# A fifth group of seven products in the second FFN projection, and the PLE product moved ahead of its gate

## Chip, cores and metric

The kernel runs on one core of a Trainium2 chip. The metric is the time of one execution on the device in microseconds (us), lower is better; a kernel's time is the median of several executions.

## What is computed

One layer of an encoder over 1024 tokens of width 1024, all in float32. In short:

```python
hn = rmsnorm(h, norm_mix_g);  z = hn @ w_in            # pooling mixer and chunked attention
h  = h + concat([a, o]) @ w_out
hn = rmsnorm(h, norm_ffn_g);  up = hn @ w_up           # 1024 x 5632
gt, val = up[..., :2816], up[..., 2816:]
gt = causal_dwconv(gt, conv_w, conv_b)                 # width 3
h  = h + (gelu(gt) * val) @ w_down                     # 2816 x 1024, the second projection
hn = rmsnorm(h, norm_ple_g)
gate = sigmoid(hn @ w_ple_gate + b_ple_gate)
h  = h + gate * (p @ w_ple)                            # p is 1024 x 256, the PLE product
out = rmsnorm(h, final_g)
```

The change concerns the second projection and what follows it.

## The kernel before

**Products.** Everything lies transposed: features on the 128 partitions, tokens along the free axis. Each float32 operand is split into a high part (ACT copies it to the type `fp32r`) and a low part (DVE subtracts); `split` (L132 to L134) does both. A product of two operands is three matmuls, high x high, high x low, low x high (`mm3`, L128 to L130). A token half is 512 columns, a PSUM bank; PSUM has eight banks.

**First projection.** The 2816 features are 22 tiles of 128, `fi` = 0 to 21. For each tile gate and value columns are computed together by seven products in the manner of Strassen instead of eight: steps `n` in the order (1, 5, 6, 2, 7, 3, 4), each 4 x 3 = 12 matmuls. `step(fi, n)` issues one, the text counts them as steps 1 to 7 of a tile by position. DVE forms sums of weight quarters (L700) and ACT and DVE split them, three products ahead. PSUM results are handed from product to product: `keep` copies one out (L785), `seed` copies a bank into another (L789), on which the next product accumulates. After step 6 (`n` = 3) the convolution and GELU run (L834 to L837), after step 7 the value factor (L842 to L851), and the tile's result Y lies in `Yb`. `up(fi, ...)` is one tile; its hooks are things to do between steps.

**Second projection.** The output rows are 8 blocks `H[d]` of 128, two token halves each. Two ways are used:

- *Plain*: for two tiles at a time, each block and half gets 2 x 3 matmuls (`down_mm`), and DVE adds the bank to `H` (`down_add`). Y and the weights `w_down` must be split first.
- *Groups of four tiles*: seven products for eight, over halves of the output features, token halves and pairs of tiles. Y goes to DRAM (`Yd`, L908), and sums of Y blocks and of weight blocks are put together by loading one block and adding others on top in DMAs of the POOL queue (L961), into one of two raw buffers for each kind ("one", "grow"; L963 loads from the SP queue). `ask` issues these loads when a buffer is free and the tiles that are read are stored; `split_next` splits the operands of the next product into the buffers `pairs` (tiles BQ and a part of R), of which there is one set; `down_next` issues one product, 4 x 2 x 3 = 24 matmuls into banks 4 to 7, adds them to H by four DVE instructions (L1008), and calls `split_next` for the next product. `H` holds sums of its quarters meanwhile, formed and undone by DVE.

Before, tiles 0 and 1 are plain (during tile 2), tiles 2 to 17 are four groups, tiles 18 and 19 and tiles 20 and 21 are plain, behind the last tile, accumulated together in PSUM. A group's seven products stand between the steps of the four tiles that follow it; those of the last group in tiles 18 and 19 alone:

```python
        for fi in range(3, 6):
            up(fi, negative(fi))
            if fi == 3:
                split_next()
        for g in range(1, 4):
            for z, fi in enumerate(group_of(g)):
                up(fi, negative(fi), {n: down_next for i, n in enumerate(steps[fi]) if (7 * z + i) % 4 == 1})
        last_at = (1, 4, 6, 8, 10, 12, 13)
```

**Gate.** Behind it come the norm of H, the gate product (8 blocks of 8 x 3 matmuls, for tokens 0 to 511, 512 to 767 and 768 to 1023 in turn), and in each of these 24 rounds, behind the gate product, the PLE product of the same block (`ple_mm`, 2 x 3 matmuls). `gate_out` takes the sigmoid (L1157), multiplies it with the PLE product in PSUM (L1158) and adds to H (L1159). The final norm and the output follow.

**Order.** TensorE executes in the order of the program text. The instructions of the other engines, their DMAs among them, are ordered by a planner when the kernel is built, by the order of the text (`tc.high_priority` moves some ahead) and by its own estimates of when their inputs are there. Each engine then executes its list in order.

Of the kernel before, what the change touches and what calls it, by code (L numbers as in the profile page):

```python
# [6 lines left out]
F32 = mybir.dt.float32  # L7
# [86 lines left out]
def trunk(tc, xT, pT, vecs, w_qk0, w_in, w_v, bias, counts, pool_w, w_out, w_up, w_down,  # L94
# [4 lines left out]
    with tc.tile_pool(name="sb", bufs=1) as sb, \  # L99
# [567 lines left out]
        rawu = [f(2 * s, 512) for s in range(4)] + [f(40, 512)]  # L667
        rawd = f(42, 512)
# [33 lines left out]
        def prepare(upto):  # L702
            while prepared[0] < min(upto, len(order)):
# [3 lines left out]
                fetch(prepared[0] + 2)  # L707
# [158 lines left out]
        b_pool = tc.tile_pool(name="b3", bufs=1)  # L866
        B = b_pool.__enter__().tile([P, 7168], F32R, name="B3")
        gv = [B[:, 2048 * s:2048 * (s + 1)] for s in range(2)]
        wd = [(B[:, 4096:5120], B[:, 5120:6144]), (B[:, 6144:7168], r(60, 1024))]

        def down_weights(fi, dst, raws=(rawd,)):
            for z in range(2):
                t = raws[z % len(raws)]
                sp.dma_start(t, w_down[fi, :, z * 512:(z + 1) * 512])
                split(t, dst[0][:, z * 512:(z + 1) * 512], dst[1][:, z * 512:(z + 1) * 512])

        def down_mm(d, h, bank, ws, gs, first=True, last=True):
            for i in range(2):
                w_, a = ws[i], gs[i]
                mm3(PS[:, bank], w_[0][:, d * P:(d + 1) * P], w_[1][:, d * P:(d + 1) * P],  # L880
                    a[:, h * 512:(h + 1) * 512], a[:, 1024 + h * 512:1024 + (h + 1) * 512],
                    first and i == 0, last and i == 1)
# [3 lines left out]

        def down(tiles, ring):
            for n in tiles:
                d, h = n % KT, n // KT
                bank = ring[n % len(ring)]  # L890
                down_mm(d, h, bank, wd, gv)
                down_add(d, h, bank)

        def up(fi, dst, hooks=None):
# [5 lines left out]
            for n in steps[fi]:  # L900
                step(fi, n)
                if hooks and n in hooks:
                    hooks[n]()
            if isinstance(dst, int):

                values_in(slice(0, SEQ), dst)
                for ts in HS:
                    sp.dma_start(Yd[fi][:, ts], Yb[:, ts])  # L908
                stored.add(fi)
                ask()  # L910
                return
# [5 lines left out]
        def downs(ring):  # L917
            def at(a, b):
                return lambda: down(range(a, b), ring)
            return {6: at(0, 4), 3: at(4, 8), 7: at(8, 12), 4: at(12, 16)}  # L920


        Yd, stored = {}, set()
        raws, pairs = {}, {}
        asked, todo = {}, []
        split_done = set()

        def group_of(g):
            return range(4 * g + 2, 4 * g + 6)
# [12 lines left out]
        def ask():  # L942
# [3 lines left out]
            for side in "wa":  # L946
                for kind in ("one", "grow"):
                    queue = todo_of[side, kind]
                    while queue:
# [5 lines left out]
                        queue.pop(0)  # L955
                        grown = n in (GROWING_W if side == "w" else GROWING_A)[1:]
# [18 lines left out]
        sequence = [(g, n) for g in range(4) for n in DOWN_ORDER]  # L975
# [20 lines left out]
        def down_next():  # L996

            g, n = sequence[ndown[0]]
            ndown[0] += 1
            fresh = n in (1, 5, 6, 7)  # L1000
# [9 lines left out]

        down_weights(0, wd[0])
        up(0, gv[0])
        up(1, gv[1], {7: lambda: down_weights(1, wd[1])})
        d_pool = tc.tile_pool(name="yd", bufs=1, space=bass.MemoryType.DRAM)
        dp = d_pool.__enter__()
        for fi in range(2, NF - 3):
            Yd[fi] = dp.tile([P, SEQ], F32, name=f"Yd{fi}")
        up(2, 1, downs((4, 5, 6, 7)))
        b_pool.__exit__(None, None, None)
        b_pool = tc.tile_pool(name="bq", bufs=1)  # L1020
        bp = b_pool.__enter__()
        B = bp.tile([P, 3072], F32R, name="BQ")
        RW = bp.tile([P, 4096], F32, name="RW")
        spots = [B[:, 1024 * z:1024 * (z + 1)] for z in range(3)] + [r(60, 1024)]
        for s, side in enumerate("wa"):
            for j in range(2):
                p_ = spots[2 * s + j]
                pairs[side, j] = p_[:, 0:512], p_[:, 512:1024]
                for q, kind in enumerate(("one", "grow")):
                    z = 4 * s + 2 * q + j  # L1030
                    raws[side, kind, j] = RW[:, 512 * z:512 * (z + 1)]
        for d in range(4):
            for a, b, op in ((H[4 + d][:, HS[0]], H[4 + d][:, HS[1]], ALU.subtract),
                             (H[d][:, HS[1]], H[4 + d][:, HS[1]], ALU.add)):
                dve.tensor_tensor(a, a, b, op)
        ask()

        def negative(fi):

            return 1 if (fi - 2) % 4 < 2 else 0  # L1040
# [11 lines left out]
        b_pool.__exit__(None, None, None)  # L1052
        b_pool = tc.tile_pool(name="b3t", bufs=1)
        B = b_pool.__enter__().tile([P, 7168], F32R, name="B3T")
        gv = [B[:, 2048 * s:2048 * (s + 1)] for s in range(2)]
        wd = [(B[:, 4096:5120], B[:, 5120:6144]), (B[:, 6144:7168], r(60, 1024))]
        for ts in HS:
            store(gv[1], ts)
        for d in range(4):
            for a, b, op in ((H[4 + d][:, HS[0]], H[4 + d][:, HS[1]], ALU.add),  # L1060
                             (H[d][:, HS[1]], H[4 + d][:, HS[1]], ALU.subtract)):
                dve.tensor_tensor(a, a, b, op)
        for ts in HS:
            sp.dma_start(rawd, Yd[18][:, ts])
            split(rawd, gv[0][:, ts], gv[0][:, 1024 + ts.start:1024 + ts.stop])
        for fi in (18, 19):
            down_weights(fi, wd[fi % 2])
# [3 lines left out]
        wd2 = [(r(8 * s, 1024), r(8 * s + 4, 1024)) for s in range(2)]  # L1071
        banks = (4, 5, 6, 7, 0, 2, 1, 3)

        nl = len(loads)
        raw_last = [(rawu[nl % 5], rawd), (rawu[(nl - 4) % 5], rawu[(nl - 1) % 5])]
        up(last_f[0], None)
        up(last_f[1], gv2[1], {1: lambda: store(gv2[0]),
                             3: lambda: down_weights(last_f[0], wd2[0], raw_last[0]),
                             4: lambda: down_weights(last_f[1], wd2[1], raw_last[1])})


        wg = [r(b, 2048) for b in (44, 52, 16, 24, 96, 104, 80, 88)]
        hp = [[(r(b, 512), r(b + 2, 512)) for b in bs]
              for bs in ((112, 116, 120, 124, 32, 36, 40, 60), (0, 4, 8, 12, 64, 68, 72, 76))]
# [3 lines left out]
        def pair(src, hi, lo):  # L1088
            t = rawg[ng[0] % 3]
            ng[0] += 1  # L1090
            sp.dma_start(t, src)
            split(t, hi, lo)
# [17 lines left out]
        for d in range(KT):  # L1110
            down_mm(d, 0, banks[d], wd, gv, True, False)
        for k in range(KT):
            pair(w_gate[k], wg[k][:, 0:1024], wg[k][:, 1024:2048])
        for d in range(KT):
            down_mm(d, 0, banks[d], wd2, gv2, False, True)
            down_add(d, 0, banks[d])
            norm_a.add(d, pool)
        for d in range(KT):
            down_mm(d, 1, banks[d], wd, gv, True, False)
            if d < 7:  # L1120
                weighted2(0, d)
        weighted2(0, 7)
        b_pool.__exit__(None, None, None)
        v_pool.__exit__(None, None, None)
        b_pool = tc.tile_pool(name="b4", bufs=1)
        B = b_pool.__enter__().tile([P, 8192], F32R, name="B4")
        pt = [B[:, 2048 * k:2048 * (k + 1)] for k in range(2)]
        wp = [B[:, 4096 + 2048 * k:4096 + 2048 * (k + 1)] for k in range(2)]
        for k in range(2):
            pair(pT[k], pt[k][:, 0:1024], pt[k][:, 1024:2048])  # L1130
            pair(w_ple[k], wp[k][:, 0:1024], wp[k][:, 1024:2048])
# [161 lines left out]
```

## Time and profile before

| | us |
|---|---|
| three executions | 1148.33, 1150.03, 1153.02 |
| median | 1150.03 |
| the profiled execution | 1150.81 |
| its span, first to last instruction | 1149.0 |

| engine | busy, us | share |
|---|---|---|
| TensorE (PE) | 1133.6 | 99% |
| VectorE (DVE) | 875.9 | 76% |
| ScalarE (ACT) | 589.8 | 51% |
| GpSimd (POOL) | 139.6 | 12% |

In rows of the profile PE is a matmul and PEld a weight load, "SPq" an issue in SyncE's queue. A row of a timeline begins with start and duration in us; an engine's idle time before the instruction, and what ended it, stand in brackets. In rows by stage each engine has its busy time and number of instructions; the granted TensorE clock, the share of the DMA engines and GB/s follow. Durations of matmuls overlap; the time of one is the distance between two starts. The same holds for DVE and ACT instructions in a row.

In the profiled execution the FFN's first group product starts at 522.41 us, the last at 930.41, and the first gate product at 1022.8. The span ends at 1149.0.

### The profile page before, as it was taken

The page shows a single profiled execution, that of the slowest core. Times are in us where ns is not written, and L with a number is a line of the kernel's source. Part 1 is how long each engine was busy: PE and PEld are TensorE (multiplying, and loading weights), DVE is VectorE, ACT ScalarE, POOL GpSimd, SP SyncE. Part 2 cuts the span into 40 slices and gives each one's busy share as a digit, 9 for nine tenths or more (in the row PEclk, how much of TensorE's full clock was granted, in tenths as well). Part 3 has the DMA queues.
Part 4 walks back from the last instruction along what each step waited for, and adds up shares of the span by engine and source line. Part 5 has one row for each costly group of instructions (what it writes and reads, how often), then busy time and mean ns, then how long its engine had stood idle before and what let it go on. Part 6 is the DMA issues. An engine that isn't in the chain of part 4 may idle for free.

```text
span 1149.0 us, 15722 instructions
## 1 busy us (share of the span) xinstructions
PE 1133.6 (99%) x5747; PEld 963.4 (84%) x5747; DVE 875.9 (76%) x1504; ACT 589.8 (51%) x1035; POOL 139.6 (12%) x179
## 2 busy tenths in 40 slices
PE   8999999999999999999999999999999999999997
PEld 7988998888888878878888888888888878888897
DVE  7678878879657887778787887787878799776543
ACT  8568677765555651444343534453444436645433
POOL 0000000083002100001201120112012200220000
PEclk9999999999999999999999999999999999999999
DMA  7110102104500120545755574557455903600012
GB/s 264 37 49 31 49 12 68 40 28 155 166 19 9 56 74 31 151 130 138 173 139 156 147 174 129 156 147 174 129 156 147 219 1 110 195 26 1 10 65 74
DMA packets 58975, 115.93 MB, mean 101 GB/s; under 512 B 6673, under 2 KB 7953, under 8 KB 58897
## 3 DMA queue, kind: packets, MB, share of 16 engines
q1 hardware_dynamic: 47232, 93.88, 24.2%
q0 software_dynamic: 11520, 20.98, 11.4%
q8 instruction: 45, 0.74, 0.3%
q14 instruction: 34, 0.27, 0.1%
q10 hardware_dynamic: 144, 0.07, 0.0%
HBM read 101.79 MB, written 13.11 MB: 100 GB/s over the span
## 4 chain that ended last, share of the span: by engine, by line
PE 92%; issue 3%; DVE 2%; ACT 2%; DMA 0%; SPq 0%; POOL 0%; POOLq 0%; DVEq 0%; ACTq 0%
PE PS L128 28%; PE PS L129 28%; PE PS L130 28%; PE PS L367 2%; PE PS L385 1%; PE PS L384 1%; PE PS L342 1%; PE PS L341 1%; DMA F<-in_w_qk 0%; PE PS L350 0%; PE PS L349 0%; PE PS L617 0%; ACT F L353 0%; DVE B L375 0%; DVE BQ L134 0%
## 5 line engine op out<-in xcount | busy, mean ns | idle before, releaser
L128 PE MATMUL PS<-R 128*128 128x512 f32 (+1 forms) x1144 | 430.1, 376 | 3.3 <-ACT PS L789 1.4
L130 PE MATMUL PS<-R 128*128 128x512 f32 (+1 forms) x1144 | 425.1, 372 | 0.0
L129 PE MATMUL PS<-R 128*128 128x512 f32 (+1 forms) x1080 | 407.1, 377 | 0.3 <-DVE R L230 0.3
L128 PEld LDWEIGHTS PS<-R 128*128 128x128 f32 x1144 | 215.6, 188 | 40.9 <-ACT PS L789 2.7
L130 PEld LDWEIGHTS PS<-R 128*128 128x128 f32 x1144 | 215.4, 188 | 37.9
L129 PEld LDWEIGHTS PS<-R 128*128 128x128 f32 x1080 | 203.6, 189 | 35.3 <-DVE R L230 0.6
L133 ACT ACTIVATE R<-F 128x512 fp32r<-128x512 f32 (+2 forms) x217 | 136.3, 638 | 186.7 <-PE PS L129 76.2
L134 DVE TENSOR_TENSOR R<-F,R 128x512 fp32r<-128x512 f32 (+2 forms) x213 | 148.2, 703 | 40.9 <-ACT R L133 39.8
L700 DVE TENSOR_TENSOR F<-F 128x512 f32<-128x512 f32 x88 | 61.6, 701 | 49.1 <-DMA F<-in_w_up 36.4
L133 ACT ACTIVATE BQ<-RW 128x512 fp32r<-128x512 f32 x72 | 42.2, 622 | 73.6 <-PE PS L129 69.5
L1008 DVE TENSOR_TENSOR F<-F,PS 128x512 f32<-128x512 f32 x112 | 74.0, 682 | 6.3 <-PE PS L130 6.1
L961 POOL DMA_DIRECT2D RW<-Yd x48 | 42.2, 879 | 212.4 <-DMA RW<-Yd 170.4
L961 POOL DMA_DIRECT2D RW<-in_w_down x32 | 28.8, 958 | 244.6 <-DMA RW<-in_w_down 141.7
L609 ACT ACTIVATE F<-F 128x512 f32<-128x512 f32 (+1 forms) x49 | 27.9, 570 | 55.5 <-DVE F L1159 28.5
L353 ACT ACTIVATE F<-F,small 128x640 f32<-128x640 f32 (+2 forms) x64 | 44.4, 693 | 21.2 <-DVE small L351 13.1
L834 ACT ACTIVATE F<-F,vec 128x1024 f32<-128x1024 f32 (+1 forms) x24 | 28.2, 1173 | 42.6 <-DVE F L809 39.0
L134 DVE TENSOR_TENSOR BQ<-RW,BQ 128x512 fp32r<-128x512 f32 x72 | 47.5, 686 | 2.2 <-ACT BQ L133 1.1
L375 DVE TENSOR_TENSOR B<-PS,B 128x640 fp32r<-128x640 f32 (+2 forms) x64 | 42.0, 656 | 9.2 <-ACT B L374 8.2
L129 PE MATMUL PS<-BQ 128*128 128x512 f32 x112 | 43.9, 392 | 2.7 <-DVE BQ L134 2.7
L374 ACT ACTIVATE B<-PS 128x640 fp32r<-128x640 f32 (+2 forms) x64 | 35.8, 560 | 17.3 <-PE PS L367 15.4
L129 PE MATMUL PS<-R,BQ 128*128 128x512 f32 x112 | 44.0, 393 | 0.0
L130 PE MATMUL PS<-R,BQ 128*128 128x512 f32 x112 | 44.0, 393 | 0.0
(195 smaller groups left out, 2008.1 us busy)
## 6 DMA issues: line engine op xcount, KB each, us to landing
F<-in_w_up SPq DMA_DIRECT2D x91, 256.0 KB, 3.7
RW<-Yd SPq DMA_DIRECT2D x48, 256.0 KB, 3.6
RW<-Yd POOLq DMA_DIRECT2D x48, 256.0 KB, 4.8
RW<-in_w_down SPq DMA_DIRECT2D x40, 256.0 KB, 2.8
Yd<-F SPq DMA_DIRECT2D x34, 256.0 KB, 2.2
RW<-in_w_down POOLq DMA_DIRECT2D x32, 256.0 KB, 6.2
F<-in_w_in SPq DMA_DIRECT2D x10, 512.0 KB, 3.5
F<-in_xT SPq DMA_DIRECT2D x16, 256.0 KB, 5.8
```

What stands on the lines that cost most here:

```text
L128: pe.matmul(ps, ahi, bhi, start=first, stop=False, skip_group_check=more)
L129: pe.matmul(ps, ahi, blo, start=False, stop=False, skip_group_check=more)
L130: pe.matmul(ps, alo, bhi, start=False, stop=last, skip_group_check=more)
L133: act.activation(hi, src, AF.Copy)
L134: dve.tensor_tensor(lo, src, rv(hi), ALU.subtract)
L353: act.activation(S[:, 0:n], S[:, 0:n], AF.Exp, bias=s_[:, 0:1], scale=-1.0, accum_out=s_[:, 1:2])
L374: act.activation(hi, pst, AF.Copy)
L375: dve.tensor_tensor(lo, pst, rv(hi), ALU.subtract)
L700: dve.tensor_tensor(rawu[to], rawu[a], rawu[b], op)
L834: act.activation(y, Gb[:, 2 + a:2 + b], AF.Identity, bias=vec[:, C_CB + fi:C_CB + fi + 1], scale=cw(2))
L961: pool.dma_start(t, src, accum_op=ALU.add)
L1008: dve.tensor_tensor(t, t, PS[:, 4 + d], ALU.subtract if n in (1, 5) else ALU.add)
```

## The change

Tiles 0 to 19 become five groups of four; only tiles 20 and 21 stay plain. The products of groups 0 to 3 stand between the steps as before (in tiles 4 to 18, and two more in tile 19), those of group 4 behind step 7 of tile 19, steps 4 and 6 of tile 20 and steps 1, 3, 5 and 7 of tile 21. `split_next` now does nothing while the loads that it reads are not yet issued, or while a split product has not been issued; it is called again at the end of a tile, behind the store and the loads. The first split of group 0 is issued behind tile 2. The raw ring of `w_up` has six buffers for five, and is filled one step further ahead.

The PLE product is computed in 512 columns ahead of the gate, for the first token half behind tile 21, for the second between the plain products of the first half; ACT copies it from PSUM to SBUF (`po`), and the multiplication by the sigmoid reads it there. Its operands are loaded and split in tile 21 (the weights behind step 4, the first half of p behind step 6) and behind it. Half of the gate weights are split behind the PLE product, at whose operands' addresses they lie. The squares of the norm ahead of the gate are summed by DVE instead of POOL, and the final norm of a token group is taken two rounds later.

```diff
-        rawu = [f(2 * s, 512) for s in range(4)] + [f(40, 512)]
-        rawd = f(42, 512)
+        rawu = [f(2 * s, 512) for s in range(4)] + [f(40, 512), f(42, 512)]
...
-                fetch(prepared[0] + 2)
+                fetch(prepared[0] + 3)
...
+                if fi > 3:
+                    split_next()
                 return
...
         def group_of(g):
-            return range(4 * g + 2, 4 * g + 6)
+            return range(4 * g, 4 * g + 4)
...
                         queue.pop(0)
+                        asked.add((side, g, n))
...
-                for g in range(4):
+                for g in range(5):
...
         def split_next():
-            if nsplit[0] == len(sequence):
+            if nsplit[0] == len(sequence) or nsplit[0] > ndown[0]:
                 return
             g, n = sequence[nsplit[0]]
+            if not all((side, g, n) in asked for side in "wa"):
+                return
...
-        down_weights(0, wd[0])
-        up(0, gv[0])
-        up(1, gv[1], {7: lambda: down_weights(1, wd[1])})
...
-        up(2, 1, downs((4, 5, 6, 7)))
...
-        for fi in range(3, 6):
+        for fi in range(4):
             up(fi, negative(fi))
...
-            if fi == 3:
+            if fi == 2:
+                for d in range(4):
+                    for a, b, op in ((H[4 + d][:, HS[0]], H[4 + d][:, HS[1]], ALU.subtract),
+                                     (H[d][:, HS[1]], H[4 + d][:, HS[1]], ALU.add)):
+                        dve.tensor_tensor(a, a, b, op)
+                ask()
                 split_next()
-        for g in range(1, 4):
-            for z, fi in enumerate(group_of(g)):
-                up(fi, negative(fi), {n: down_next for i, n in enumerate(steps[fi]) if (7 * z + i) % 4 == 1})
-        last_at = (1, 4, 6, 8, 10, 12, 13)
-        up(18, 2, {n: down_next for i, n in enumerate(steps[18]) if i in last_at})
-        up(19, None, {n: down_next for i, n in enumerate(steps[19]) if 7 + i in last_at})
+        places = [(1, 5), (2, 6), (3,), (0, 4)]
+        for fi in range(4, NF - 3):
+            up(fi, negative(fi), downs(fi, places[fi % 4]))
+        up(NF - 3, negative(NF - 3), downs(NF - 3, (0, 4, 6)))
...
+        late = [rawu[(nl + z) % 6] for z in (0, 1)]
...
+        def ple_weights():
+            for k in range(2):
+                for z in HS:
+                    late_pair(w_ple[k, :, z], wp[k][0][:, z], wp[k][1][:, z])
+        def ple_rows(h):
+            for k in range(2):
+                late_pair(pT[k, :, HS[h]], *pt[h][k])
...
+        up(last_f[0], None, downs(last_f[0], (3, 5)))
+        hooks = downs(last_f[1], (0, 2, 4, 6))
+        for n, fn in ((1, lambda: store(gv2[0])), (2, ple_weights), (3, lambda: ple_rows(0)),
+                      (4, lambda: late.extend(rawu[(nl + z) % 6] for z in (2, 3, 4, 5)))):
+            hooks.setdefault(n, []).insert(0, fn)
+        up(last_f[1], gv2[1], hooks)
...
+        def ple_mm(h, d, bank):
+            ds_ = slice(d * P, (d + 1) * P)
             for k in range(2):
+                mm3(PS[:, bank], wp[k][0][:, ds_], wp[k][1][:, ds_], *pt[h][k], k == 0, k == 1)
+            act.activation(po[8 * h + d], PS[:, bank], AF.Copy)
+
+        down_weights(last_f[0], wd2[0])
+        down_weights(last_f[1], wd2[1])
+        ple_rows(1)
+        for d in range(KT):
+            ple_mm(0, d, ple_banks[d])
+        gate_weights(range(4))
+        for d in range(KT):
+            down_mm(d, 0, banks[d], wd2, gv2)
+            down_add(d, 0, banks[d])
+            norm_a.add(d)
+            ple_mm(1, d, banks[(d + 4) % 8])
...
+        gate_weights(range(4, 8))
+        for d in range(KT):
+            down_mm(d, 1, banks[d], wd2, gv2)
+            down_add(d, 1, banks[d])
...
-            dve.tensor_tensor(t, PS[:, ple_bank, 0:b - a], t, ALU.mult)
+            dve.tensor_tensor(t, po[8 * (a // 512) + d][:, a % 512:a % 512 + b - a], t, ALU.mult)
...
-                ple_mm(dz, *groups[gz], ple_banks[z % 2])
-                gate_out(dz, *groups[gz], gate_banks[z % 3], ple_banks[z % 2], zt[z % 4])
+                gate_out(dz, *groups[gz], gate_banks[z % 3], zt[z % 4])
...
-            if g and d == 0:
+            if g and d == 2:
                 last[g - 1].sums()
-            if g and d == 1:
+            if g and d == 3:
                 last[g - 1].rows()
```

More of the change, by code (lines that the diff above doesn't have):

```diff
@@ L865, in trunk, with down_mm @@
         t_pool.__exit__(None, None, None)
[L866 to L877, printed above, removed]
+        d_pool = tc.tile_pool(name="yd", bufs=1, space=bass.MemoryType.DRAM)
+        dp = d_pool.__enter__()
+        Yd = {fi: dp.tile([P, SEQ], F32, name=f"Yd{fi}") for fi in range(NF - 2)}
+        def down_mm(d, h, bank, ws, gs):
             for i in range(2):
@@ L1022, in trunk @@
[L1022 to L1031, printed above, removed]
@@ L1052, in trunk @@
[L1052 to L1062, printed above, removed]
@@ L1063, in trunk @@
[L1063 to L1067, printed above, removed]
+            if fi == 1:
+                b_pool = tc.tile_pool(name="bq", bufs=1)
+                bp = b_pool.__enter__()
+                B = bp.tile([P, 3072], F32R, name="BQ")
+                RW = bp.tile([P, 4096], F32, name="RW")
+                spots = [B[:, 1024 * z:1024 * (z + 1)] for z in range(3)] + [r(60, 1024)]
+                for s, side in enumerate("wa"):
+                    for j in range(2):
+                        p_ = spots[2 * s + j]
+                        pairs[side, j] = p_[:, 0:512], p_[:, 512:1024]
+                        for q, kind in enumerate(("one", "grow")):
+                            z = 4 * s + 2 * q + j
+                            raws[side, kind, j] = RW[:, 512 * z:512 * (z + 1)]
+                ask()
@@ L1108, in normed2 @@
             weighted2(1, k, t)
[L1110 to L1131, printed above, removed]
```

99 lines of the change are left out of this document (46 added, 53 removed).

## The prediction

> **What bounds the kernel now.** First the page (span, engines, chain), then busy time by stage.
>
> ```profile
> span 1149.0 us, 15722 instructions
> ...
> PE 1133.6 (99%) x5747; PEld 963.4 (84%) x5747; DVE 875.9 (76%) x1504; ACT 589.8 (51%) x1035; POOL 139.6 (12%) x179
> ...
> PE 92%; issue 3%; DVE 2%; ACT 2%; DMA 0%; SPq 0%; POOL 0%; POOLq 0%; DVEq 0%; ACTq 0%
> ```
>
> ```profile
> 500.00:600.00 100.00, 100.00 (x443) 82.81 (x442) 78.79 (x120) 43.83 (x71) 13.97 (x16) 1.00 0.56 146
> ...
> 854.25:927.69 73.44, 73.44 (x326) 60.81 (x324) 61.72 (x97) 32.10 (x53) 13.97 (x16) 1.00 0.65 154
> ```
>
> TensorE is both the longest chain (92%) and busy throughout; DVE is second, 79% in the regular stretch (500 to 600) and 84% where the last group's products stand closer (854 to 928: 61.72 of 73.44). So a product removed pays its full issue time, unless a wait fills its place. Next: the waits of TensorE (the two that count beside the longest), and the timeline around the longest.
>
> ```profile
> PE PS L128 <- ACT PS L789: 1.4, 2, 0.8
> ...
> PE PS L128 <- ACT F L785: 0.6, 2, 0.4
> ```
>
> ```profile
> 925.65 0.39 PE L128 MATMUL PS<-R,BQ 128*128 128x512 f32 x1
> ...
> 930.41 0.39 PE L128 MATMUL PS<-BQ 128*128 128x512 f32 x1
> 933.51 0.50 PE L129 MATMUL PS<-BQ 128*128 128x512 f32 x1 [2.72 <-DVE BQ L134]
> ...
> 934.79 0.63 PE L130 MATMUL PS<-R,BQ 128*128 128x512 f32 x1
> ...
> 937.35 0.54 PE L130 MATMUL PS<-R,BQ 128*128 128x512 f32 x1
> ...
> 940.49 0.39 PE L128 MATMUL PS<-R 128*128 128x512 f32 x1
> ```
>
> From 925.65 to 930.41 lie 21 issues: 4.76/21 = 0.2267 us per 512-column matmul. An up product (12) takes 2.72 us, a group product (24) 5.44. The product at 930.41, the last of the last group, takes 10.08 us to 940.49: 4.64 too many. Of that 2.72 is the wait for the last split of its weights; then, from 934.79 to 937.35, six issues take 0.427 each, nearly twice the normal, which with the restarts is the rest. The Trainium skill (TensorE: Matmul & The Clock Gate, "What's actually happening") halves the clock after an idle window of about 3.4 us; here 2.72 us were enough, so the measurement decides; by the rule this overrun would cost its wait alone, and removing it would bring 2.7 to 3.1.
>
> **The change part by part.** *Fewer matmuls.*
>
> ```profile
> L129 PE MATMUL PS<-BQ 128*128 128x512 f32 x112 | 43.9, 392 | 2.7 <-DVE BQ L134 2.7
> ...
> L128 PE MATMUL PS<-B3T 128*128 128x512 f32 x32 | 12.4, 389 | 0.0
> ```
>
> Six rows of 112 like the first make 672 matmuls: four groups of seven products of 24. Two plain tiles take 8 row blocks x 2 halves x 2 tiles x 3 = 96 (B3T: 32 for each of the three lines). Before: 672 + 3 x 96 = 960. After: 5 x 168 + 96 = 936. So 24 less, all in dense stretches: **-5.44 us**.
>
> *PLE product ahead of the gate.*
>
> ```profile
> L128 PE MATMUL PS<-B x48: 283/283/486, 1035.0 to 1139.2; 128*128 128x256 f32 x32, 128*128 128x512 f32 x16
> ```
>
> ```profile
> 1138.73 0.28 PE L130 MATMUL PS<-R 128*128 128x256 f32 x1
> 1138.85 0.28 PE L128 MATMUL PS<-B 128*128 128x256 f32 x1
> ...
> 1139.05 0.47 ACT L1157 ACTIVATE F<-PS,vec 128x256 f32<-128x256 f32 x1 [0.58 <-PE PS L130]
> ...
> 1139.45 0.28 PE L130 MATMUL PS<-B 128*128 128x256 f32 x1
> ...
> 1139.84 0.42 DVE L1158 TENSOR_TENSOR F<-PS,F 128x256 f32<-128x256 f32 x1 [1.46 <-PE PS L130]
> ```
>
> A 256-column matmul takes 0.120 (five issues from 1138.85 to 1139.45). Today three lines of 16 x 0.2267 + 32 x 0.120 = 22.40 us, 21.68 of it ahead of the last gate product; afterwards 96 x 0.2267 = 21.76, all ahead: +0.08. At the end the multiplication waits until 1139.84 for the PLE product, though the sigmoid was done at 1139.52; with its operand in SBUF it starts 0.03 behind the sigmoid: -0.29. Together **-0.21**. Its price is 16 copies out of PSUM on ACT:
>
> ```profile
> L785 ACT ACTIVATE F<-PS 128x512 f32<-128x512 f32 x44 | 25.7, 584 | 13.8 <-PE PS L130 13.8
> ...
> F<-in_w_up SPq DMA_DIRECT2D x91, 256.0 KB, 3.7
> ```
>
> At the 0.584 of such a copy they are 9.3 us, beside 192 matmuls (PLE and the plain tiles), 43.5 us of TensorE, with eight banks in turn: nothing. Uncovered, one copy would hold its bank for 0.6.
>
> *The late split.* The last group loses its 2.72 us window: its products stand two up products (5.44 us) apart or more. **-4.64**, if no new wait comes.
>
> *The first group's first split.*
>
> ```profile
> 493.36 0.63 ACT L133 ACTIVATE R<-RW 128x512 fp32r<-128x512 f32 x1 [4.36 <-DMA RW<-Yd]
> ```
>
> ```profile
> 493.91 0.39 PE L130 MATMUL PS<-R 128*128 128x512 f32 x1
> 495.05 0.50 PE L128 MATMUL PS<-R 128*128 128x512 f32 x1 [0.76 <-ACT PS L789]
> ```
>
> Today it is issued behind tile 3, which it reads: ACT stands 4.36 us before a load, the seed copy queues behind it, and TensorE's step from 493.91 to 495.05 is 1.14 instead of 0.23. In the new order it reads tiles 0 and 1 and is issued behind tile 2, a tile (19 us) after their stores: **-1.0** with the slow first matmul. The other short waits (1.4 - 0.76 by the seed, 0.6 by L785) I leave: the burst of first loads on SP moves from behind tile 2 to behind tile 1, and the sixth raw buffer fetches a step earlier; between -1.4 and +1.4, taken as 0.
>
> *The new dense end.* In tiles 4 to 18 products stand where they stood, by position in their groups. New is group 4 (tiles 16 to 19): products behind step 7 of tile 19, steps 4 and 6 of tile 20, steps 1, 3, 5, 7 of tile 21. Five have a 5.44 us window in which ACT and DVE split four operand halves, as the operands are single. How long that takes today (last split of a window, then the product that waits for it):
>
> ```profile
> 886.54 0.69 DVE L134 TENSOR_TENSOR R<-RW,R 128x512 fp32r<-128x512 f32 x1
> 889.61 0.39 PE L128 MATMUL PS<-BQ 128*128 128x512 f32 x1
> ...
> 899.01 0.69 DVE L992 SCALAR_TENSOR_TENSOR R<-RW,R 128x512 fp32r<-128x512 f32 x1
> 900.49 0.39 PE L128 MATMUL PS<-BQ 128*128 128x512 f32 x1
> ...
> 920.64 0.69 DVE L992 SCALAR_TENSOR_TENSOR BQ<-RW,BQ 128x512 fp32r<-128x512 f32 x1
> 921.25 0.69 DVE L992 SCALAR_TENSOR_TENSOR R<-RW,R 128x512 fp32r<-128x512 f32 x1
> 922.25 0.39 PE L128 MATMUL PS<-BQ 128*128 128x512 f32 x1
> ...
> 933.37 0.69 DVE L134 TENSOR_TENSOR R<-RW,R 128x512 fp32r<-128x512 f32 x1
> ```
>
> Slack 2.4, 0.8 and 0.3 us: the splits took 3.0, 4.6 and 5.1 of 5.44. The short window's last split ended at 934.06, 6.4 us after its start at 927.69. DVE instructions in a row follow each other at 0.60 (920.64, 921.25). In the regular stretch four tiles and seven products take 28 x 2.72 + 7 x 5.44 = 114.2 us of TensorE and, at 78.8%, 90.0 of DVE; the products' 56 DVE instructions (four adds and four splits each) are 33.6 of these, so a tile has 14.1. Tile 21 then has 14.1 + 4 x 8 x 0.60 = 33.3, and eight more halves, 4.8, for the store of tile 20 and the six PLE splits that lie in it: 38.1 of 40.8 us, 93% against 84% above. What is late next is therefore a split again: a window overruns by 0 (the three above did not) up to 6.4 - 5.44 = 0.9, with 0.2 for the restart (at 495.05 above 1.14 - 0.23 - 0.76), five times 5.6 in all. I take 0.5 each, nearer to the windows of the same length: **+2.5**.
>
> *The load in front of group 4's second product.*
>
> ```profile
> 636.65 0.39 PE L128 MATMUL PS<-BQ 128*128 128x512 f32 x1
> ...
> 639.95 0.93 SPq L908 DMA_DIRECT2D Yd<-F  x2
> ...
> 642.19 0.32 SPq L963 DMA_DIRECT2D RW<-Yd  x1
> ...
> 644.86 0.63 ACT L991 ACTIVATE R<-RW 128x512 fp32r<-128x512 f32 x1 [1.81 <-DMA RW<-Yd]
> ...
> 645.53 0.69 DVE L992 SCALAR_TENSOR_TENSOR R<-RW,R 128x512 fp32r<-128x512 f32 x1 [0.99 <-ACT R L991]
> ...
> 652.97 0.39 PE L128 MATMUL PS<-BQ 128*128 128x512 f32 x1
> ```
>
> Tile 9 ends on TensorE two up products before 636.65, at 631.2. Store, load and split are done at 646.2, 15.0 us later; the product comes 21.8 us after the tile. For tile 19 it comes after one group product and four steps: 5.44 + 10.88 = 16.3. Slack 1.3. The change places the split behind the tile's store, so ACT is not held longer than the 1.8 us seen; behind it queue the up splits and seed copies, for TensorE. Between 0 and 2; I take **+0.5**.
>
> *PLE operands.* Six loads through two raw buffers from step 4 of tile 21 on, each pair a load (3.7 above) and its two splits on DVE (1.2, more behind others), three rounds of 5 in the 19 us that tile 21 still lasts. On SP they stand behind the last weight loads, before the plain tiles' weights only. Between 0 and 3 late: **+0.5**.
>
> *Edits taken as nothing.* The half sums of H are 16 DVE instructions before and after. The last four gate weights share addresses with the PLE operands, so their splits start 10.9 us before the gate; DVE has 12 us of work there (four subtractions and eight adds at 0.60, four splits of twice that), but the fourth is needed only by the last eighth of a 5.44 us product. Between 0 and 1.5, hidden by that.
>
> **Sum.** -5.44 - 0.21 - 4.64 - 1.0 = -11.3 without a new wait; with +3.5 of them -7.8. The profiled execution took 1150.81 (span 1149.0 and 1.8 around it), 0.8 above the median of three, 1150.03. On the median: **1142.2**.
>
> **The rivals.** *All windows hold*: DVE takes the new splits in its free fifth; for it speaks that only the 2.72 us window was missed; against it 0.3 us of slack and a fuller tile 21. 1150.0 - 11.3 = 1138.7, or 1137.3 if the other short waits go too. *Nothing left*: windows overrun like the worst one (5.6), PLE operands 3 late, the load 2: 10.6, so 1149.3. *Slower*: TensorE's clock drops at every window. If a split takes over about 8 us, the wait reaches the 2.7 us at which the half clock was seen, and each window costs the 4.64 of today's; five times that, 23.2, gives 1150.0 - 11.3 + 23.2 = 1161.9. Slower by 0.5% begins at 17.1 us of new waits, 3.4 per window. For it speaks DVE at 93%; against it that no split took over 6.4. By the skill's 3.4 us rule the same waits would not cost the half clock.
>
> **How the numbers follow.** About 0.5%, 5.75 us, is what a measurement of this kernel can tell from no change: 1144.3 to 1155.8. Forecast 0.52 (1140 to 1146, a fifth of it above 1144.3), all windows hold 0.20, nothing left 0.16, slower 0.12. Faster 0.42 + 0.20 = 0.62, same 0.10 + 0.16 = 0.26, slower 0.12. The range runs from the case without a wait, 1137.3, to a little above the third, 1150; it leaves out the slower one and edges.
>
> **What would show it.** 5747 - 24 - 48 = 5675 matmuls; 140 in each BQ row; no ACT wait of 4 us before tile 4; no group product over 7 us; TensorE's waits in tiles 20 and 21 short and ended by DVE's splits; in the tail the multiplication right behind the sigmoid. Wrong would be: half-clock issues (0.427) at several products, a wait over 2 us at the PLE product or the first gate product, or ACT standing before a load with a seed copy behind it.

## The result and the profile after

| | before | after |
|---|---|---|
| median, us | 1150.43 (20 runs) | 1146.74 (20 runs) |
| lowest to highest, us | 1148.26 to 1154.72 | 1143.54 to 1150.71 |
| span of the profiled execution, us | 1149.0 | 1145.1 |

The ratio is 0.9964, 95% interval 0.9952 to 0.9976: faster by 3.7 us, where 7.8 were forecast. The page of the changed kernel, its parts on the span, the engines and the chain:

```profile
span 1145.1 us, 15750 instructions
...
PE 1129.9 (99%) x5675; PEld 958.2 (84%) x5675; DVE 888.2 (78%) x1541; ACT 604.7 (53%) x1068; POOL 146.8 (13%) x192
...
PE 93%; issue 2%; ACT 2%; DMA 1%; DVE 1%; SPq 0%; POOL 0%; POOLq 0%; DVEq 0%; ACTq 0%
```

The 5675 matmuls are the forecast 72 fewer. The rest is in what TensorE waits for; these are the changed kernel's rows that answer to the two of before:

```profile
PE PS L129 <- DVE BQ L973: 2.7, 2, 1.6
PE PS L128 <- ACT F L784: 2.1, 1, 2.1
...
PE PS L128 <- ACT PS L788: 0.7, 1, 0.7
PE PS L128 <- ACT BQ L972: 0.3, 1, 0.3
```

Before, one wait of 2.72 us stood at the last group product. Now two group products wait (2.7 in all and 0.3), and a copy of ScalarE (L784, `keep`) is 2.1 us late once. By stage, the changed kernel around the last group's fourth to seventh products (columns as before: PE, PEld, DVE, ACT, POOL, clock):

```profile
943.00:957.00 14.00, 12.87 (x57) 10.35 (x56) 12.96 (x20) 6.66 (x10) 5.24 (x6) 1.00 0.85 140
957.00:997.70 40.70, 38.78 (x163) 31.30 (x163) 34.27 (x55) 20.46 (x35) 5.25 (x6) 0.96 0.60 150
```

DVE has 34.27 of 40.70 there, 84%, and TensorE's clock was lowered for a part of the second stage. Three places matter.

**Tile 0.** ScalarE's timeline, then SyncE's queue, then TensorE's, all of the changed kernel:

```profile
390.27 0.58 ACT L784 ACTIVATE F<-PS 128x512 f32<-128x512 f32 x1
394.75 0.63 ACT L133 ACTIVATE BQ<-RW 128x512 fp32r<-128x512 f32 x1 [3.90 <-DMA RW<-in_w_down]
395.29 0.61 ACT L133 ACTIVATE R<-F 128x512 fp32r<-128x512 f32 x1
395.81 0.58 ACT L784 ACTIVATE F<-PS 128x512 f32<-128x512 f32 x1
```

```profile
390.89 0.80 SPq L942 DMA_DIRECT2D RW<-in_w_down  x2
```

```profile
396.44 0.63 PE L128 MATMUL PS<-R 128*128 128x512 f32 x1 [2.08 <-ACT F L784]
396.87 0.63 PE L129 MATMUL PS<-R 128*128 128x512 f32 x1
...
399.43 0.63 PE L129 MATMUL PS<-R 128*128 128x512 f32 x1
```

The split of the first group's first weight is written behind tile 2 in the text, but it hangs on a load alone, and the planner put both into tile 0, 40 us before the 434.8 at which it runs in experiment 2, where it is tied. The load is issued at 390.89, ScalarE stands 3.90 us before it, and a split and the copy that TensorE needs queue behind. TensorE idles 2.08 us and then issues at 0.427 instead of 0.2267 eight times: 4.3 us with the small wait at 390.

**The fourth product.** TensorE, ScalarE and POOL of the changed kernel:

```profile
955.55 0.50 PE L129 MATMUL PS<-BQ 128*128 128x512 f32 x1 [1.13 <-DVE BQ L973]
```

```profile
952.08 0.63 ACT L972 ACTIVATE R<-RW 128x512 fp32r<-128x512 f32 x1 [2.46 <-DMA RW<-Yd]
```

```profile
944.18 0.86 POOL L940 DMA_DIRECT2D RW<-Yd  x1 [1.85 <-issue]
944.79 1.15 POOL L940 DMA_DIRECT2D RW<-in_w_down  x1
946.55 0.88 POOL L940 DMA_DIRECT2D RW<-Yd  x1 [0.61 <-issue]
```

The last half of its Y operand is a chain of adding loads; the last is issued at 946.55, behind an adding load for the fifth product's weights (944.79), and ScalarE gets it at 952.08, 1.96 us before the product's first start at 954.04. The split ends late and the wait with its restart costs 1.4 us.

**The sixth product.** ScalarE, SyncE's queue and TensorE of the changed kernel:

```profile
967.42 0.62 ACT L133 ACTIVATE R<-F 128x512 fp32r<-128x512 f32 x1
974.16 0.63 ACT L133 ACTIVATE R<-F 128x512 fp32r<-128x512 f32 x1 [6.12 <-DMA F<-in_w_down]
976.01 0.63 ACT L133 ACTIVATE R<-F 128x512 fp32r<-128x512 f32 x1 [1.22 <-DMA F<-in_w_down]
976.55 0.62 ACT L133 ACTIVATE BQ<-RW 128x512 fp32r<-128x512 f32 x1
```

```profile
967.02 1.10 SPq L1041 DMA_DIRECT2D F<-in_w_down  x2
```

```profile
977.74 0.49 PE L128 MATMUL PS<-BQ 128*128 128x512 f32 x1 [0.33 <-ACT BQ L972]
979.83 0.50 PE L129 MATMUL PS<-BQ 128*128 128x512 f32 x1 [1.59 <-DVE BQ L973]
980.16 0.48 PE L130 MATMUL PS<-BQ 128*128 128x512 f32 x1
980.45 0.63 PE L128 MATMUL PS<-R,BQ 128*128 128x512 f32 x1
...
986.80 0.39 PE L128 MATMUL PS<-R 128*128 128x512 f32 x1
```

ScalarE stands 6.12 us before a load that took 7.1 us from its issue at 967.02, to split a weight of the *plain* tiles, wanted some 34 us later (behind the last group product and the eight PLE products, at about 1008.6). The splits of the sixth product, whose buffers the fifth product had left by 971.8 (24 issues from 966.37), begin at 976.55. The product takes 986.80 - 977.74 = 9.06 us instead of 5.44, and 0.5 is lost ahead of it: 4.1.

**The balance.** Adding up all starts of TensorE that follow each other by more than the issue time of their shape, from 380 us to the last gate matmul, gives 8.9 us lost before and 11.5 after. Gone are 4.6 at 930, 1.8 between 482 and 495 and 0.7 at 971; new are 4.3, 1.4 and 4.1. Ahead of that, where nothing was changed, about 0.5 us less is lost. With -5.36 for the matmuls, -0.28 in the gate's tail, -0.37 in the final stores and +2.1 lost, the span falls by 3.9.

### The profile page after: what moved, and what is told of

The parts are those of the page before. It is cut to its first block, busy times and chain, and to the rows that moved or that the text cites. A ratio compares the mean times of both kernels' runs of the same rounds, so it can differ in the third digit from the quotient of the medians.

```text
span 1145.1 us, 15750 instructions
## 1 busy us (share of the span) xinstructions
PE 1129.9 (99%) x5675; PEld 958.2 (84%) x5675; DVE 888.2 (78%) x1541; ACT 604.7 (53%) x1068; POOL 146.8 (13%) x192
## 4 chain that ended last, share of the span: by engine, by line
PE 93%; issue 2%; ACT 2%; DMA 1%; DVE 1%; SPq 0%; POOL 0%; POOLq 0%; DVEq 0%; ACTq 0%
PE PS L128 28%; PE PS L129 28%; PE PS L130 28%; PE PS L367 2%; PE PS L385 1%; PE PS L384 1%; DMA F<-in_w_down 1%; PE PS L342 1%; PE PS L341 1%; DMA F<-in_w_qk 0%; PE PS L350 0%; PE PS L349 0%; PE PS L617 0%; DMA RW<-in_w_down 0%; ACT F L353 0%
## 5 line engine op out<-in xcount | busy, mean ns | idle before, releaser
L128 PE MATMUL PS<-R 128*128 128x512 f32 (+1 forms) x1176 | 443.2, 377 | 2.8 <-ACT F L784 2.1
L130 PE MATMUL PS<-R 128*128 128x512 f32 (+1 forms) x1176 | 438.4, 373 | 0.0
L129 PE MATMUL PS<-R 128*128 128x512 f32 (+1 forms) x1112 | 420.8, 378 | 0.3 <-DVE R L230 0.3
L128 PEld LDWEIGHTS PS<-R 128*128 128x128 f32 x1176 | 222.1, 189 | 40.7 <-ACT F L784 2.8
L130 PEld LDWEIGHTS PS<-R 128*128 128x128 f32 x1176 | 222.1, 189 | 39.1
L129 PEld LDWEIGHTS PS<-R 128*128 128x128 f32 x1112 | 210.0, 189 | 37.1 <-DVE R L230 0.9
L133 ACT ACTIVATE R<-F 128x512 fp32r<-128x512 f32 (+2 forms) x225 | 141.3, 637 | 186.1 <-PE PS L129 76.4
L133 ACT ACTIVATE BQ<-RW 128x512 fp32r<-128x512 f32 x90 | 52.8, 623 | 85.5 <-PE PS L129 78.8
L990 DVE TENSOR_TENSOR F<-F,PS 128x512 f32<-128x512 f32 x140 | 92.3, 680 | 4.4 <-PE PS L130 4.3
L940 POOL DMA_DIRECT2D RW<-Yd x60 | 52.4, 873 | 267.2 <-DMA RW<-Yd 215.2
L940 POOL DMA_DIRECT2D RW<-in_w_down x40 | 36.1, 951 | 227.1 <-DMA RW<-in_w_down 190.1
L134 DVE TENSOR_TENSOR BQ<-RW,BQ 128x512 fp32r<-128x512 f32 x90 | 59.1, 684 | 5.6 <-ACT BQ L133 4.3
L129 PE MATMUL PS<-BQ 128*128 128x512 f32 x140 | 54.9, 392 | 2.7 <-DVE BQ L973 2.7
L128 PE MATMUL PS<-BQ 128*128 128x512 f32 x140 | 54.8, 392 | 0.3 <-ACT BQ L972 0.3
L128 PE MATMUL PS<-R,BQ 128*128 128x512 f32 x140 | 55.0, 393 | 0.0
L129 PE MATMUL PS<-R,BQ 128*128 128x512 f32 x140 | 54.9, 392 | 0.0
L130 PE MATMUL PS<-BQ 128*128 128x512 f32 x140 | 54.8, 391 | 0.0
L130 PE MATMUL PS<-R,BQ 128*128 128x512 f32 x140 | 54.7, 391 | 0.0
```

The source lines that it names most:

```text
L128: pe.matmul(ps, ahi, bhi, start=first, stop=False, skip_group_check=more)
L129: pe.matmul(ps, ahi, blo, start=False, stop=False, skip_group_check=more)
L130: pe.matmul(ps, alo, bhi, start=False, stop=last, skip_group_check=more)
L133: act.activation(hi, src, AF.Copy)
L134: dve.tensor_tensor(lo, src, rv(hi), ALU.subtract)
L940: pool.dma_start(t, src, accum_op=ALU.add)
```

## The experiments

`tc.issue_after(x)` makes the planner place the instructions within it behind `x` on their engine. Line numbers shift by 2 to 20 in these kernels (`mm3` at L130 to L132, `keep` L788, `seed` L794).

**1. The plain tiles' splits late.** In the changed kernel, the splits of the plain tiles' weights, and of the second PLE operand, queue behind the splits of the last group's last product.

```diff
+        with tc.issue_after(split_mark[0]):    # last split of the last group
             down_weights(last_f[0], wd2[0])
             down_weights(last_f[1], wd2[1])
             ple_rows(1)
```

> The changed kernel with one thing altered: ACT's splits of the plain tiles' weights and of the second half of p are queued behind the splits of the last group's last product; their loads stay where they are (some from 967 us on). Theory A: ACT's wait of 6.1 us for a plain weight goes, so the splits of group 4's sixth product start when its fifth is done, and the step of 4.2 us lost near 977 us goes: about 1142.5, ratio 0.9927. Rival C (DVE, 93% busy in tile 21, is what makes the windows overrun): the loss near 977 shrinks by less than 1.5 us, or moves to the next window or to the PLE product. The losses at 394 and near 954 stay.

Measured: 1144.98 us, ratio 0.9941 [0.9927, 0.9955]. Around the sixth product ScalarE of this kernel now has

```profile
970.84 0.63 ACT L135 ACTIVATE BQ<-RW 128x512 fp32r<-128x512 f32 x1 [3.63 <-issue]
```

and no TensorE wait is left in the sixth product: the 4.1 us are gone. So it was the plain weight's split, not DVE. By the ratios the gain is 2.6 us, not 4.1; how often the half clock follows in other executions (experiment 8) may be part of that, which is not shown. The loss in tile 0 stays, here as 1.69 us idle without a half-clock issue behind it.

**2. The first group's first split late.** It queues behind tile 2's last seed copy.

```diff
+            with tc.issue_after(seeds[-1]) if (g, n) == (0, 1) else nullcontext():
                 for side in "wa":
```

> The changed kernel with one thing altered: ACT's splits for the first product of group 0 are queued behind the last seed copy of tile 2; their loads stay where they are (issued from 390.9 us on). Theory A (ACT stands in its list before a split whose load has not landed, and the copies that TensorE needs queue behind it): the wait of 2.08 us at 394 us and the half-clock issues behind it go, 4.2 us, so about 1142.5, ratio to the kernel before 0.9927, and the two waits near 954 and 977 us stay. Rival B (the early burst of loads delays the weights of the first projection, and TensorE waits for those): the wait at 394 stays within 0.5 us, time unchanged at 1146.7, since the loads are not moved.

Measured: 1143.73 us, ratio 0.9932 [0.9919, 0.9945]. The loss at 394 is gone, but one of about the same size comes up at 402: 2.1 us for the seed copy, then half-clock issues. The ratio is near what theory A gave, yet the profile says B for this place: moving the split alone uncovers the loads. Of the 2.1 us by which the profiled execution's span is shorter, 1.7 come from the sixth product, which waited 1.58 us here without the half clock; so the ratio's nearness to theory A is luck, and where the median's 3.7 us come from is not shown.

**3. Both.** 

> Both alterations together. Theory A: they add up, 4.2 + 4.2 = 8.4 us, so about 1138.3, ratio 0.9894; the waits left in the second projection are 1.4 us near 954 us and 0.95 at the first seed of tile 1. Rivals B and C: between 1142 and 1146.7.

Measured: 1141.34 us, ratio 0.9916 [0.9902, 0.993], less than expected for the same reason. Its TensorE and DVE at 402:

```profile
404.95 0.63 PE L130 MATMUL PS<-R 128*128 128x512 f32 x1 [2.16 <-ACT PS L794]
405.37 0.63 PE L131 MATMUL PS<-R 128*128 128x512 f32 x1
```

```profile
397.69 0.69 DVE L703 TENSOR_TENSOR F<-F 128x512 f32<-128x512 f32 x1 [1.54 <-DMA F<-in_w_up]
...
399.63 0.69 DVE L703 TENSOR_TENSOR F<-F 128x512 f32<-128x512 f32 x1 [1.24 <-DMA F<-in_w_up]
```

DVE waits twice for a `w_up` load that shares the DMA engines with the first group's loads, the GELU of tile 0 comes late, and the seed copy stands behind it on ScalarE.

**4. The first loads late too.** The first group's loads on SyncE queue behind the stores of tile 1.

```diff
+                with tc.issue_after(stores[-1]):
                     ask()
```

> The version with both splits late, and the first group's weight loads, the burst that the sync engine issues while tile 0 is split, queued behind the stores of tile 1 as well. Theory A (the loads of the first weights delay the up weights of tile 2 while they are in flight together, so its GELU and its seed come late: the 2.16 us wait with half clock at 402 us): that wait shrinks to under 1 us without half-clock issues, worth about 3 us against the version with both splits late (some 1138.5 us, ratio to the kernel before about 0.989). Theory B (the wait at 402 us comes from the scalar engine's own work, its table load and GELU, whatever is in flight): the wait stays at about 2 us and the time stays at 1141. Rival C: the burst only moves, and one of the tiles 3 to 5 waits 1 to 2 us instead: 1140.

Measured: 1141.31 us, ratio 0.9912 [0.9896, 0.9928]. At 402 the wait is 0.7 us, as in the kernel before, and no half-clock issue follows: theory A for the place. But 1.5 us are lost anew near 449, much as C said, and the ratio hardly moves: the wait that was taken away does not cost its 4.0 us in every execution (experiment 8).

**5. The order of the adding loads.** On the POOL queue the fifth product's weights go behind the fourth product's Y (in the expectation products bear their `n`: 6 is the fifth by place, 4 the fourth).

```diff
+                                    with tc.issue_after(added[-1]) if behind else nullcontext():
                                         pool.dma_start(t, src, accum_op=ALU.add)
```

> The version before this one, and the accumulating loads of group 4's sixth product (made by the pool engine's queue) queued behind those of its fourth product's activation side. Theory A (the wait at about 953 us, 1.1 to 2.3 us, is a chain of accumulating loads that is in the queue behind loads needed later): the wait falls to under 0.5 us, 1 to 1.5 us in time. Theory B (the chain is bound by the landing of each load, 5 to 6 us, not by its place in the queue): the wait stays within 0.5 us of what it was, and the time too.

Measured: 1140.56 us, ratio 0.9902 [0.9884, 0.992], profiled execution 1138.86. ScalarE has the operand 3.65 us before the product's first start (951.57), not 1.96, and TensorE does not wait in the last group at all. ScalarE and the stage of tile 21 in this kernel:

```profile
947.92 0.63 ACT L985 ACTIVATE R<-RW 128x512 fp32r<-128x512 f32 x1 [0.77 <-DMA RW<-Yd]
```

```profile
953.00:994.00 41.00, 41.00 (x183) 33.95 (x182) 37.42 (x60) 25.00 (x42) 5.25 (x6) 1.00 0.65 170
```

DVE is busy 91% and TensorE 41.00 of 41.00: the full DVE holds every window. The order was tested once more, beside the version without it:

> The version with the accumulating loads reordered once more, because the wait at 953 us without the reorder came out between 0.4 and 2.3 us in four executions. Theory A (the order of the queue sets it): again no wait over 0.3 us there, and a median 0.7 to 1.2 us below the version without the reorder. Theory B (the wait only varies): 0.5 us or more there in this execution, and the medians agree within 0.5 us.

> The version without the reorder beside it. Theory A: a wait of 0.4 to 2.3 us at 953 us and 0.7 to 1.2 us more in the median. Theory B: no difference in the median.

Measured: 1139.57 us, ratio 0.9883 [0.9864, 0.9902], with the order; 1140.49, ratio 0.9892 [0.9874, 0.991], without. At the fourth product TensorE waited 0 in both executions with it, 1.06 and 1.28 us in both without. The medians differ by 0.75 and 0.92, as theory A has it, though the intervals overlap.

**6. The kernel before, last group respaced.** The old kernel with the short window taken away: how much of the gain needs no fifth group?

```diff
-        last_at = (1, 4, 6, 8, 10, 12, 13)
+        last_at = (1, 3, 5, 7, 9, 11, 13)
```

> The kernel before with the last group's products at steps 2, 4, 6 of tile 18 and 1, 3, 5, 7 of tile 19 (they stood at 2, 5, 7 and 2, 4, 6, 7), so that no window is shorter than 5.44 us; four groups and the PLE product at the gate as before. Theory A: the loss of 4.6 us at 930 us goes; the second product comes 2.7 us sooner and waits for its load by 0 to 1.5 us, so about 1146.5, ratio 0.9966. That would be as fast as the changed kernel, and a pair with e3 to read off what the fifth group and the PLE product bring by themselves: 5.6 us. Rival C (DVE): the overrun moves to the other windows and the time stays within 1.5 us of before.

Measured: 1148.5 us, ratio 0.9977 [0.9967, 0.9988]. The 4.6 us at 930 are gone; 1.2 and 0.9 return at two other products, 0.5 more at 497, and some 1.6 more at 484, 585 and 814 together. The profiled execution, 1151.58, is the slowest of the twelve. By the medians 2.6 us of the late split's 4.64 are gained.

**7. The same, first split late.** First only emitted a tile later, then tied in the queue as in experiment 2.

> The kernel before with its last group's products respaced, and the first group's first split a tile later, without the fifth group and with the PLE product behind the gate as it was. The wait of 1.28 us at 495 us goes (the scalar engine no longer stands 4 us before a tile's load): about 1.4 us less than the respaced version alone, 1146.5 to 1147, ratio 0.996. If group 0 of products then comes too close to group 1, two or three waits of 0.5 us appear in tiles 5 to 8 and nothing is won. Its distance to the two kernels above is the fifth group and the PLE product alone, without their side effects: 5.65 us by the count of matmuls and the tail.

> The same as the run before of the old kernel, but the first group's first split is now tied in the scalar engine's queue behind the first seed copy of tile 4, not only emitted later. Theory A (the prediction's term of 1.0 us: the seed copy stands behind a split that waits 4.3 us for a load): the wait of 1.0 to 1.3 us at 494 us goes and nothing takes its place, 1.2 us in the trace against the version without this tie, ratio to the kernel before about 0.9968. Theory B (the up weights or the GELU are late there for themselves): TensorE still waits over 0.7 us there.

Measured: 1148.84 us, ratio 0.9979 [0.9966, 0.9993], and 1147.29, ratio 0.9964 [0.9948, 0.998]. The first edit did nothing: the planner put the split into the same place, where ScalarE again stood 4.29 us and TensorE 1.03. So its distance to the fifth-group kernels, which its expectation meant as a reading, is none. Tied in the queue, the wait at 494 is gone and nothing takes its place there: theory A. Mended so, the old kernel is as fast as the changed one; both mended, they stand at 0.9902 / 0.9964 = 0.9938 (no interval, as they ran in different rounds), 7.1 us, or 9.3 by the second measurement of the mended kernel (0.9883), for the 5.65 of the fifth group and the PLE product by count. From 380 us to the last gate matmul the profiled executions lose 3.4 and 5.9 us to waits, so part of the rest may lie there.

**8. The half clock.** The changed kernel and the version of experiment 3, each executed once more.

> The changed kernel once more, to see the half clock in another execution. If the half clock follows from the length of the idle time (theory A), the wait of 2.1 us at 394 us and that of 1.6 us at 978 us again bring eight or nine issues of 0.427 each. If it hangs on where the wait falls in a window that runs by itself (theory B), one of the two places shows the wait without them, and the time is 1.7 us shorter for each that is missing.

> The version with both splits late once more. Theory A (the length of the idle time decides): half-clock issues again behind the wait of 2.2 us at 402 us and again none behind that of 2.3 us at 953 us cannot both follow from a length, so one of them must come out otherwise here. Theory B (phase of a window): either place can show them, and the waits themselves stay within 0.3 us of 2.2 and 2.3.

Measured: 1145.85 and 1139.86 us. The changed kernel waits 2.43 us at 394 with the half clock, and 1.15 us at the sixth product without it. The version with both splits late waits 1.70 us at 402, without half clock, and 0.43 at the fourth product where it had been 2.32. So the waits themselves vary by up to 1.9 us, against theory B's 0.3, and these two runs alone can't refute theory A, since every wait without the half clock is a shorter one here. Across kernels the length does not decide, as TensorE's rows of experiment 7's second kernel and of experiment 3 show, which are to be held against 2.08 above:

```profile
921.88 0.50 PE L131 MATMUL PS<-BQ 128*128 128x512 f32 x1 [2.11 <-DVE BQ L997]
922.22 0.39 PE L132 MATMUL PS<-BQ 128*128 128x512 f32 x1
922.45 0.40 PE L130 MATMUL PS<-R,BQ 128*128 128x512 f32 x1
```

```profile
956.16 0.50 PE L131 MATMUL PS<-BQ 128*128 128x512 f32 x1 [2.32 <-DVE BQ L980]
956.50 0.40 PE L132 MATMUL PS<-BQ 128*128 128x512 f32 x1
```

Both idles are longer than 2.08, and from the second start behind them on the distance is 0.23.

What the half clock goes with stands in the traces' records of the granted clock. Up to the last gate matmul they show six halvings in all, each 3.41 us long. In the changed kernel they begin at 396.65 and 980.33, with one more at 1140.76 behind the gate; the second and third lie 171 and 218 steps of 3.413 us behind the first, so the steps run through the whole execution. Cut into these steps, each of the fourteen traces has TensorE idle for 1.92 to 2.68 us of the step ahead of a halving, and for at most 1.69 us of any step with none behind it. The rows by stage of the changed kernel, then of experiment 3, in each the step with the wait (or its two) and the clock behind:

```profile
393.24:396.65 3.41, 1.33 (x9) 0.92 (x8) 1.24 (x2) 1.90 (x4) 0.00 (x0) 1.00 0.83 281
396.65:400.06 3.41, 3.41 (x9) 2.63 (x9) 3.15 (x6) 1.86 (x4) 1.98 (x2) 0.50 0.85 273
```

```profile
951.29:954.71 3.42, 2.55 (x12) 1.77 (x10) 0.13 (x1) 2.02 (x4) 1.73 (x2) 1.00 0.85 168
954.71:958.12 3.41, 1.96 (x9) 1.62 (x10) 3.31 (x6) 1.07 (x3) 0.88 (x1) 1.00 1.00 197
```

The wait of 2.08 us lies whole in one step; that of 2.32 is cut by a border into 0.87 and 1.45, and the clock stays. So the traces bear out theory B's window. The place of a wait in it changes from one execution to the next: experiment 3's wait at 402 begins 1.04 us into a step, the one of its repetition 3.17.

## Why the prediction was right, and where it was not

The sign and the range were right, the size was half. By the prediction's own bands 1146.7 falls into "same", which had a chance of 0.26: it lies above 1144.3 and above the 1140 to 1146 of its main case (by the ratio it is 1145.9 on the prediction's base, at that case's edge), though the interval over 20 runs tells the two kernels apart. That the range held owes something to its width. By its own terms, in the profiled execution:

| term | predicted, us | measured, us |
|---|---|---|
| fewer matmuls | -5.44 | -5.44 |
| PLE product | -0.21 | -0.20 |
| late split of the last group | -4.64 | -4.64 |
| first group's first split, and the first loads | -1.0 | -1.8 + 4.3 |
| five windows | +2.5 | 1.4 + 4.1 |
| load before the second product | +0.5 | 0 |
| PLE operands | +0.5 | 0 |
| not in the sum: 971, ahead of the FFN, last stores | 0 | -1.6 |
| sum | -7.8 | -3.9 |

*Matmuls, PLE.* Right in count and place. The multiplication stands right behind the sigmoid, as foreseen; ScalarE and DVE of the changed kernel:

```profile
1135.78 0.47 ACT L1143 ACTIVATE F<-PS,vec 128x256 f32<-128x256 f32 x1 [0.49 <-PE PS L130]
```

```profile
1136.29 0.43 DVE L1144 TENSOR_TENSOR F<-V,F 128x256 f32<-128x256 f32 x1 [1.08 <-ACT F L1143]
```

It ran 0.83 us behind the start of the last gate matmul (1135.46), 1.11 before (1138.73 to 1139.84).

*The steps that failed.* First, "the burst of first loads on SP moves from behind tile 2 to behind tile 1 [...] taken as 0", together with "is issued behind tile 2, a tile (19 us) after their stores". Both took the place in the text for the place in the queue. The weight half of that split reads no store, so nothing held it behind tile 2. It was issued in tile 0, ahead of its load's landing: +4.3 for the 1.8 that went, 3.5 above the term and outside the bounds of 1.4 given there. Experiments 2 to 4 show two parts of it, the split and then the loads, each of which alone leaves a wait.

Second, the windows' price. The total of 5.5 happens to lie at the upper bound of 5.6, but by another mechanism. The prediction reasoned from DVE at 93%; three of the five windows took no extra time, and experiment 5 has none late at DVE 91%. The other two were late by what ScalarE stood before: a load issued 7 us before it landed (experiment 1), and a chain in the wrong order (experiment 5). On the plain tiles' weights the text said only that the PLE loads stand before them on SP; that their splits stand on ScalarE ahead of the group's was not costed.

*The signs it named.* ScalarE before a load with a needed copy behind it was on the list of what would be wrong, and it is what happened. No ScalarE wait of 4 us stands before tile 4 any more, except that of 3.90 in tile 0; one product went over 7 us, the sixth with 9.06, where none was expected to.

*The rivals.* "All windows hold" gave 1138.7: the version of experiment 5 ran at 1140.56 and 1139.57, against 1151.46 and 1152.83 for the kernel before beside it, ratios that put it at 1136.6 to 1138.8 on the prediction's base. That rival named the right state of the windows, for a kernel whose queues are in order. "Slower" was right in its mechanism at one product, where the half clock came behind an idle time of 1.59 us, 0.33 just ahead of it, but not at every window. Its condition, a wait of 2.7 us, was not the right one (experiment 8).

## What to carry to other kernels

Where a planner orders the queues, a step's place in the text bounds nothing unless a dependence or an explicit tie does: before costing a moved split, ask what is the earliest it could be issued, what load it would then stand before, and who queues behind it on that engine. A wait on an in-order engine for data that is needed late is paid by what is needed now; tie the late work behind the urgent work. Its loads may then be what delays the urgent ones; tying them as well took that wait away here, but a smaller one came up and the time hardly moved. A busy share of 91% did not make windows late here; the order of the work did.

## What the runs showed of the hardware

TensorE issued at 0.427 us instead of 0.2267 after waits of 1.59 (with 0.33 just ahead), 2.08, 2.13, 2.16, 2.43 and, before, 2.72 us, and not after 1.58, 1.69, 1.70, 2.11 and 2.32. Each time the half clock lasted 3.41 us. What it went with was how much of one step of 3.413 us was idle: 1.92 us or more brought it, 1.69 or less did not (experiment 8); where between them the border lies, and whether other kernels have the same one, is not shown. The Trainium skill (TensorE: Matmul & The Clock Gate, "What's actually happening") has a free-running window of some 3.4 us, whose start is not tied to the kernel; the traces agree, with steps of 3.413 us. It has the half clock after at least one idle window; here a window that was idle for 1.92 of its 3.41 us was enough, so the measurement decides. A wait thus costs about 1.7 us more, half of 3.41, in some executions than in others.

A 256 KB load of SyncE's that took 2.5 us with little else in flight (kernel before, issue 961.27, DMA share 0.34) took 7.1 us (changed kernel, issue 967.02, DMA share 1.02) beside adding loads and Y loads. Execution varied too: the same wait at the fourth product was 2.32 and 0.43 us in two executions of one kernel.
